# Gate and up projections by seven products of half blocks (Strassen), the residual kept in DRAM between uses, the down projection in three row groups

## The chip, the cores and the metric

One core of a Trainium2 chip runs the whole program. The metric is the device time of one execution, in microseconds (us). PE is the matrix engine (TensorE), ACT the scalar engine, DVE the vector engine, POOL the GpSimd engine; SP issues the DMAs.

## The reference, cut to what matters

Two layers over 576 tokens (64 of a running stream, 512 of a new one), everything in fp32. Each layer is FFN, mixer, FFN, with a norm before and after each; the four FFNs are what the change is about.

```python
D_MODEL, D_FF, DEPTH = 1024, 2816, 2

def _rmsnorm(x, g):
    y = x32 * lax.rsqrt(jnp.mean(x32 * x32, axis=-1, keepdims=True) + EPS)
    return (y * g.astype(jnp.float32)).astype(x.dtype)

def _swiglu(x, w_gate, w_up, w_down):
    return (jax.nn.silu(x @ w_gate) * (x @ w_up)) @ w_down

def _trunk(x, ...):
    for l in range(DEPTH):
        h = _rmsnorm(x, ng[0])
        x = x + 0.5 * _rmsnorm(_swiglu(h, ffn_w_gate[l, 0], ffn_w_up[l, 0], ffn_w_down[l, 0]), ng[1])
        h = _rmsnorm(x, ng[2])
        ...   # mixer: latent attention, HGRN2, chunk MLP, w_out
        x = x + _rmsnorm(mix, ng[3])
        h = _rmsnorm(x, ng[4])
        x = x + 0.5 * _rmsnorm(_swiglu(h, ffn_w_gate[l, 1], ffn_w_up[l, 1], ffn_w_down[l, 1]), ng[5])
```

## The kernel before

All activations are held transposed: a tile of 128 features by 576 tokens, so 1024 features are eight tiles (index k, 0 to 7). The residual `x` lives in eight fixed tiles of the pool `const`; everything else of this size comes from the pool `slots` (54 tiles of 128x576). The tokens are worked on in two column halves, `HALF`: 320 and 256 wide.

A product in fp32 is made of three matmuls (`three`, L138): weight and activation are each split into a high part of type fp32r and a low part. For a weight chunk of 128x1024 (`chunk`, L112) the load is a DMA on SP's queue into `wraw` (3 buffers), the high part `wh` an ACT copy (L120), the low part `wl` a DVE subtraction (L121); `whi` and `wlo` have 7 buffers each. `split` (L129) does the same to activations: `hh`/`hl` for the norm's output, `gh`/`gl` for the gated values. PSUM has 6 banks of tag `mm` and 2 of tag `sm`.

An FFN (`ffn`, L304) runs over 22 unit columns f of 128 hidden features. For each f, `unit` (L294) makes 48 matmuls for the gate and 48 for the up projection (8 k, 2 halves, 3 each), and `evac` takes them out of PSUM: times the norm's factor `rbc` (DVE L319), Silu (ACT L320), gate times up (DVE L321), split. The first two f, four chunks, are special: they run half by half (`units`, `together`), paced by the norm ahead of them, and their weights are loaded ahead. After 11 units the down projection takes the first 11 row blocks as one accumulation group and puts its result into `d` (SBUF); after 22 the second group is added. Chunks of down hold 256 columns and up to 4 row blocks. The last two column tiles of the second group run half by half, so that half 0's closing norm can be worked on while PE does half 1.

That norm is `post` (L221): the squared sums over features (ones-matmul, POOL power for the root), then per k on DVE `d` times gain times factor (L231), `x` + `d` (L234), and `pre` (L171) for the next stage: high part on ACT, low part on DVE (L136), squares on ACT, their sum `acc` on POOL (L182). Such small work is written as generators and interleaved into the matmul stream by counted PE time; the framework's scheduler then fixes each engine's order. Each engine runs its own order strictly in sequence.

Of the kernel before, what the change touches and what calls it, by code (L numbers as in the profile page):

```python
# [31 lines left out]
HALF = ((0, 320, (0, 1, 2)), (320, 256, (3, 4)))  # L32
# [11 lines left out]
class Net:  # L44
# [11 lines left out]
    def mul(self, out, lhsT, rhs, start, stop):  # L56
# [5 lines left out]
        self.nc.tensor.matmul(out, lhsT, rhs, start=start, stop=stop)  # L62
# [85 lines left out]
    def colsum(self, acc, tiles):  # L148
        ps = self.sm("ss")
        for j, i in enumerate(tiles):  # L150
            self.mul(ps[:, j:j + 1], acc[:, tcol(i):tcol(i) + P], self.ones[:, 0:1], start=True, stop=True)
        return ps

    def spread(self, r, tiles):
        ps = self.sm("bc")
        c = 0
        for j, i in enumerate(tiles):
            w = twid(i)
            self.flip(ps[:, c:c + w], r[:w, j:j + 1].to_broadcast([w, P]))
            c += w  # L160
        return ps

    def new_h(self):
        self.hh = [self.slot("hh", F32R) for _ in range(KT)]
        self.hl = [self.slot("hl", F32R) for _ in range(KT)]
        self.acc = self.slot("acc")
        self.rbc = self.slot("rbc")
        self.rn = self.small("rn", 5, 2)
        self.rn2 = self.small("rn2", 5, 2)

    def pre(self, half, k, gcol):  # L171
        nc = self.nc
        c0, n, _ = HALF[half]
        sl = slice(c0, c0 + n)
        xs = self.x[k][:, sl]
        self.split(self.hh[k][:, sl], self.hl[k][:, sl], xs, scale=gcol)
# [7 lines left out]
    def pre_stats(self, half, wait, sums=None):  # L184
        nc = self.nc
        c0, n, tiles = HALF[half]
        nt = len(tiles)
        t0 = tiles[0]
        rn, rn2, rbc, acc = self.rn, self.rn2, self.rbc, self.acc
        yield wait  # L190
        ps = self.colsum(acc, tiles) if sums is None else sums[:, t0:t0 + nt]
        m = self.small("m", 5)
# [5 lines left out]
        bc = self.spread(r, tiles)  # L198
        nc.scalar.activation(rbc[:, c0:c0 + n], bc[:, :n], AF.Copy)
        self.stats_done.add(half)  # L200

    def post_factor(self, half, acc, deferred):
        nc = self.nc
        tiles = HALF[half][2]
        nt = len(tiles)
        t0 = tiles[0]
        ps = self.colsum(acc, tiles)
        m = self.small("m", 5)
# [6 lines left out]
        p = self.small("p", 5)  # L215
# [5 lines left out]
    def post(self, half, d, acc, gpost, gpre, deferred):  # L221
        nc = self.nc
        c0, n, tiles = HALF[half]
# [17 lines left out]
    def after(self, half, d, acc, gpost, gpre, deferred):  # L241
# [1050 lines left out]
```

## Time and profile before

| | |
|---|---|
| device time, median of 3 runs | 2378.94 us (2377.78 to 2379.38) |
| span of the profiled execution, first to last instruction | 2377.5 us |
| PE busy | 2310.5 us, 97%, 16805 matmuls |
| DVE busy | 1146.5 us, 48% |
| ACT busy | 890.2 us, 37% |
| POOL busy | 217.9 us, 9% |
| mean granted PE clock | 0.991 of full speed |
| DMA | 182.76 MB, mean 77 GB/s |

The profile is of one execution; the page gives no other time of it than its span, which is 1.4 us under the median of the timed runs. "Busy" is the time in which an engine had at least one instruction running. The program's stages in the profiled execution: FFN 1 to about 440 us, mixer 1 to about 750 us, FFN 2 to about 1185 us, FFN 3 to about 1615 us, mixer 2 to about 1930 us, FFN 4 to the end.

### The profile page before, as it was taken

The numbers are of one execution on the slowest core, as the hardware profiler recorded it, in microseconds if no ns is written. First come the engines' busy times: TensorE is split into PE (matmuls) and PEld (weight loads), VectorE is DVE, ScalarE is ACT, GpSimd is POOL, SyncE is SP. The second block draws the span as 40 slices with busy tenths as digits, with TensorE's granted clock in tenths as the row PEclk, the third lists the DMA queues.
The fourth block names the chain that finished last, engine by engine and source line by source line (L and its number), as shares of the span: only waits on it lengthen the run. The fifth ranks groups of instructions, "written<-read, shape, count | busy, mean of one in ns | idle before, by whom it ended". The sixth has DMA issues, their size and how long they took to land.

```text
span 2377.5 us, 39904 instructions
## 1 busy us (share of the span) xinstructions
PE 2310.5 (97%) x16805; PEld 2257.1 (95%) x16805; DVE 1146.5 (48%) x2189; ACT 890.2 (37%) x1657; POOL 217.9 (9%) x230
## 2 busy tenths in 40 slices
PE   9999999998899999999999999999988999999998
PEld 8999999887799999999999999998877999999998
DVE  5332333788666532343473223337886574323333
ACT  6222222465555322232342222224646543222222
POOL 0000000333301000000020000003332020000000
PEclk9999999999999999999999999999999999999999
DMA  6223222122110422322232232222121214222211
GB/s 187 81 74 95 81 82 79 50 78 71 60 54 28 116 76 76 98 81 68 75 89 82 71 98 80 83 87 62 39 71 56 63 32 117 76 87 82 86 65 41
DMA packets 278344, 182.76 MB, mean 77 GB/s; under 512 B 13539, under 2 KB 270805, under 8 KB 278165
## 3 DMA queue, kind: packets, MB, share of 16 engines
q1 hardware_dynamic: 278164, 180.21, 25.3%
q8 instruction: 132, 2.16, 0.4%
q14 instruction: 48, 0.39, 0.1%
HBM read 175.96 MB, written 4.23 MB: 76 GB/s over the span
## 4 chain that ended last, share of the span: by engine, by line
PE 82%; DVE 10%; ACT 3%; POOL 3%; issue 2%; DMA 0%; SPq 0%; POOLq 0%; DVEq 0%; ACTq 0%
PE u L62 46%; PE d L62 24%; PE wo L62 4%; DVE zb L546 2%; PE sc L62 1%; DVE hl L136 1%; PE n L62 1%; DVE wl L121 1%; DVE x L234 1%; PE oT L62 1%; POOL gr L145 1%; PE q L62 1%; DVE d L231 1%; DVE at L561 1%; PE k L62 1%
## 5 line engine op out<-in xcount | busy, mean ns | idle before, releaser
L62 PE MATMUL u<-hl,wh 128*128 128x320 f32 (+1 forms) x3040 | 904.2, 298 | 2.6 <-DVE hl L136 2.6
L62 PE MATMUL u<-hh,wh 128*128 128x320 f32 (+1 forms) x3040 | 904.0, 299 | 1.9 <-DVE on L674 1.4
L62 PE MATMUL u<-hh,wl 128*128 128x320 f32 (+1 forms) x3040 | 902.4, 297 | 0.0
L120 ACT ACTIVATE wh<-wr 128x1024 fp32r<-128x1024 f32 (+1 forms) x334 | 344.5, 1032 | 756.3 <-issue 397.1
L121 DVE TENSOR_TENSOR wl<-wr,wh 128x1024 fp32r<-128x1024 f32 (+1 forms) x334 | 402.4, 1206 | 431.5 <-ACT wh L120 431.0
L62 PEld LDWEIGHTS u<-hl,wh 128*128 128x128 f32 x3040 | 580.0, 191 | 4.0 <-DVE hl L136 3.6
L62 PEld LDWEIGHTS u<-hh,wh 128*128 128x128 f32 x3040 | 578.6, 191 | 3.1 <-ACT mh L132 1.8
L62 PEld LDWEIGHTS u<-hh,wl 128*128 128x128 f32 x3040 | 579.7, 191 | 0.0
L62 PE MATMUL d<-gh,wh 128*128 128x320 f32 (+1 forms) x1408 | 418.7, 297 | 0.0
L62 PE MATMUL d<-gh,wl 128*128 128x320 f32 (+1 forms) x1408 | 417.0, 296 | 0.0
L62 PE MATMUL d<-gl,wh 128*128 128x320 f32 (+1 forms) x1408 | 416.7, 296 | 0.0
L62 PEld LDWEIGHTS d<-gl,wh 128*128 128x128 f32 x1408 | 267.3, 190 | 0.0
L62 PEld LDWEIGHTS d<-gh,wh 128*128 128x128 f32 x1408 | 267.2, 190 | 0.0
L62 PEld LDWEIGHTS d<-gh,wl 128*128 128x128 f32 x1408 | 267.2, 190 | 0.0
L321 DVE TENSOR_TENSOR t<-t,u 128x320 f32<-128x320 f32 (+1 forms) x176 | 79.6, 454 | 354.2 <-PE u L62 313.2
L145 POOL TENSOR_TENSOR p<-m,mhalf 128x3 f32<-128x3 f32 (+2 forms) x14 | 13.1, 936 | 1827.2 <-DVE m L212 1622.6
L319 DVE TENSOR_TENSOR t<-u,rbc 128x320 f32<-128x320 f32 (+1 forms) x176 | 79.8, 455 | 110.9 <-PE u L62 110.9
L320 ACT ACTIVATE t<-t 128x320 f32<-128x320 f32 (+1 forms) x176 | 76.5, 436 | 136.3 <-DVE t L319 136.3
L133 DVE TENSOR_TENSOR gl<-t,gh 128x320 fp32r<-128x320 f32 (+1 forms) x176 | 79.8, 455 | 39.7 <-ACT gh L132 39.7
L132 ACT ACTIVATE gh<-t 128x320 fp32r<-128x320 f32 (+1 forms) x176 | 76.6, 436 | 42.8 <-DVE t L321 42.8
L62 PE MATMUL n<-wh,hh 128*128 128x512 f32 (+1 forms) x240 | 92.2, 384 | 0.0
L62 PE MATMUL n<-wl,hh 128*128 128x512 f32 (+1 forms) x240 | 88.2, 368 | 0.0
(297 smaller groups left out, 2549.9 us busy)
## 6 DMA issues: line engine op xcount, KB each, us to landing
wr<-ffn_w_gate SPq DMA_DIRECT2D x88, 512.0 KB, 3.8
wr<-ffn_w_up SPq DMA_DIRECT2D x88, 512.0 KB, 3.8
wr<-ffn_w_down SPq DMA_DIRECT2D x64, 512.0 KB, 3.4
wr<-w_in SPq DMA_DIRECT2D x30, 512.0 KB, 3.8
wr<-ffn_w_down SPq DMA_DIRECT2D x32, 384.0 KB, 3.1
wr<-w_out SPq DMA_DIRECT2D x16, 512.0 KB, 3.4
xn<-x_prompt SPq DMA_DIRECT2D x4, 512.0 KB, 5.3
out_y_p<-xr SPq DMA_DIRECT2D x8, 256.0 KB, 2.1
```

The costliest lines, as they stand in the source:

```text
L62: self.nc.tensor.matmul(out, lhsT, rhs, start=start, stop=stop)
L120: nc.scalar.activation(hi[:, :a * b], raw[:, :a * b], AF.Copy)
L121: nc.vector.tensor_tensor(lo[:, :a * b], raw[:, :a * b], hi[:, :a * b].bitcast(F32), op=ALU.subtract)
L132: nc.scalar.activation(hi, src, AF.Copy)
L133: nc.vector.tensor_tensor(lo, src, hi.bitcast(F32), op=ALU.subtract)
L136: nc.vector.scalar_tensor_tensor(lo, src, scale, hi.bitcast(F32), op0=ALU.mult, op1=ALU.subtract)
L145: self.nc.gpsimd.tensor_tensor(out, m, self.mhalf[:, :n], op=ALU.pow)
L231: nc.vector.scalar_tensor_tensor(d[s][:, sl], d[s][:, sl], gpost[s], bc[:, :n], op0=ALU.mult, op1=ALU.mult)
L319: nc.vector.tensor_tensor(t[:, sl], pg[:, :n], self.rbc[:, sl], op=ALU.mult)
L320: nc.scalar.activation(t[:, sl], t[:, sl], AF.Silu)
L321: nc.vector.tensor_tensor(t[:, sl], t[:, sl], pu[:, :n], op=ALU.mult)
L546: nc.vector.tensor_tensor(zo, qv[rs, :, h:], ev[rs, :, h:], op=ALU.mult)
```

## The change

**Halves.** Both column halves are now 288 wide. The sums over columns use three runs of 128 columns per half (`RUNS`).

**Seven products.** The first two unit columns stay as they are. The other twenty go in ten pairs (f, f+1) through the new `seven`: the weight is seen as 2x2 blocks (features 0-3 or 4-7 of k, unit f or f+1), the activation as 2x2 blocks (k half, column half), and Strassen's scheme makes seven block products instead of eight. Each product is 24 matmuls of 288 columns (gate and up, 4 k, 3 parts), so a pair takes 168 matmuls where two units took 192. What is added for it: four DVE additions of weights per pair (L478, L480, L488, L497, 128x1024 each), splits of the seven weight tiles p1 to p7, and copies and additions on the way out of PSUM: ACT copies L487, L496, L503, DVE L511, L518, L520, L527, L529, L531, L536, L538, L539, two Silus of 576 columns. The weights come in four tiles per pair, each by two DMAs of 256 KB.

**Sums of activations.** The combinations t1 to t4 of activation blocks are made once per FFN by the new `combine`, after the second half of the first units: 16 ACT copies of 288 columns from `x`, 8 DVE additions of 576 columns, 8 splits of 576 columns.

**Down.** Three groups of 6, 8 and 8 row blocks; a chunk is 128 columns by the group's rows; the gated values are kept unsplit (`g`) and split at their group's start. The last group does its last three column tiles half by half.

**Residual.** `x` lives in `slots` (now 57; `const` loses its eight tiles): `stow` writes it to DRAM once the next stage's activations are made, `recall` loads it at the last group of down or of w_out. `wraw` has 6 buffers.

```diff
-HALF = ((0, 320, (0, 1, 2)), (320, 256, (3, 4)))
+W2 = T // 2
+HALF = ((0, W2), (W2, W2))
+RUNS = (((0, 64), (64, P), (W2 - P, P)), ((192, P), (320, P), (448, P)))
+GROUPS = ((0, 6), (6, 14), (14, 22))
...
+    def ffn(self, l, j, gpost, gpre, gain, nxt, packed):
...
+        ops = self.combine(gain)
+        self.until(lambda: 1 in self.stats_done)
+        for f in (0, 1):
+            evac(f, 1, o[2 * f][1], o[2 * f + 1][1])
+        for f in range(2, NF, 2):
+            self.seven(f, wg, wu, ops, g, rbc)
...
+        for a, (g0, g1) in enumerate(GROUPS):
+            first, last = a == 0, a == len(GROUPS) - 1
+            for f in range(g0, g1):
+                gh[f], gl[f] = self.slot("gh", F32R), self.slot("gl", F32R)
+                self.split(gh[f], gl[f], g.pop(f))
+            if last:
+                acc = self.slot("acc2")
+                self.recall()
...
+            tail = KT - 3 if last else KT
+            for m in range(tail):
+                run(m, self.cols(wd, m * P, P, g0, g1 - g0), (0, 1))
...
+    def combine(self, gain):
+        for q in range(2):
+            b = []
+            for kp in (q, q + 2):
+                for hf in range(2):
+                    c0, n = HALF[hf]
+                    t = self.slot("b")
+                    for e in range(2):
+                        k = 2 * kp + e
+                        nc.scalar.activation(t[:, e * n:(e + 1) * n], self.x[k][:, c0:c0 + n], AF.Copy, scale=gain[k])
+                    b.append(t)
+            b11, b12, b21, b22 = b
+            def part(name, src, scale=None):
+                o = self.slot("th", F32R), self.slot("tl", F32R)
+                self.split(*o, src, scale=scale)
+                ops[name].append(o)
+            nc.vector.tensor_tensor(b11, b11, b12, op=ALU.subtract)
+            part("t1", b11)
+            nc.vector.tensor_tensor(b11, b11, b22, op=ALU.add)
+            part("t2", b11, -1.0)
+            nc.vector.tensor_tensor(b22, b22, b12, op=ALU.subtract)
+            part("t3", b22)
+            nc.vector.tensor_tensor(b21, b11, b21, op=ALU.subtract)
+            part("t4", b21)
+        self.stow()
...
+    def seven(self, f, wg, wu, ops, g, rbc):
...
+        def product(w, b, ps, start):
+            for e in range(2):
+                for k in range(4):
+                    c = e * 512 + k * P
+                    h = ops[b][k // 2]
+                    s = slice((k % 2) * W2, (k % 2 + 1) * W2)
+                    self.three(ps[e][:, :W2], w[0][:, c:c + P], w[1][:, c:c + P], h[0][:, s], h[1][:, s],
+                               start and k == 0, k == 3, not start)
+                    self.tick()
...
+        a11, a21, a22 = load(0, f), load(0, f + 1), load(4, f + 1)
+        p1 = part(a11)
+        s = self.wraw.tile([P, 1024], F32, name=self.name("ws"), tag="wr")
+        nc.vector.tensor_tensor(s, a21, a22, op=ALU.add)
+        p5 = part(s)
+        nc.vector.tensor_tensor(a21, a21, a11, op=ALU.add)
+        a12 = load(4, f)
+        X = [self.mm("X"), self.mm("X")]
+        product(p1, "b11", X, True)
+        s1 = [self.slot("s1"), self.slot("s1")]
+        for e in range(2):
+            nc.scalar.activation(s1[e][:, A], X[e][:, :W2], AF.Copy)
+        nc.vector.tensor_tensor(s, s, a11, op=ALU.add)
+        p6 = part(s)
+        Q = [self.mm("Q"), self.mm("Q")]
+        product(p5, "t1", Q, True)
+        s5 = self.slot("s5")
+        for e, h in enumerate((A, B)):
+            nc.scalar.activation(s5[:, h], Q[e][:, :W2], AF.Copy)
+        nc.vector.tensor_tensor(s, s, a12, op=ALU.add)
+        p3 = part(s)
+        product(p6, "t2", X, False)
+        for e in range(2):
+            nc.scalar.activation(s1[e][:, B], X[e][:, :W2], AF.Copy)
+        p7 = part(a21)
+        product(p3, "b22", Q, False)
+        g[f] = self.slot("g")
+        t = [g[f], s1[1]]
+        for e in range(2):
+            nc.vector.tensor_tensor(t[e][:, B], s1[e][:, B], Q[e][:, :W2], op=ALU.add)
+        p2 = part(a12)
+        product(p7, "t3", X, False)
+        for e, h in enumerate((A, B)):
+            nc.vector.tensor_tensor(s5[:, h], s5[:, h], X[e][:, :W2], op=ALU.add)
+        nc.vector.scalar_tensor_tensor(g[f + 1][:, B], s5[:, A], -1.0, rbc[:, B], op0=ALU.mult, op1=ALU.mult)
+        p4 = part(a22)
+        R = [self.mm("R"), self.mm("R")]
+        product(p2, "b21", R, True)
+        for e in range(2):
+            nc.vector.tensor_tensor(t[e][:, A], s1[e][:, A], R[e][:, :W2], op=ALU.add)
+        nc.vector.tensor_tensor(t[0], t[0], rbc, op=ALU.mult)
+        nc.scalar.activation(t[0], t[0], AF.Silu)
+        nc.vector.tensor_tensor(g[f], t[0], t[1], op=ALU.mult)
+        product(p4, "t4", X, False)
+        nc.vector.scalar_tensor_tensor(u[:, A], X[0][:, :W2], -1.0, rbc[:, A], op0=ALU.mult, op1=ALU.mult)
+        nc.scalar.activation(u, u, AF.Silu)
+        nc.vector.scalar_tensor_tensor(u[:, B], s5[:, B], -1.0, u[:, B], op0=ALU.mult, op1=ALU.mult)
+        nc.vector.scalar_tensor_tensor(u[:, A], X[1][:, :W2], -1.0, u[:, A], op0=ALU.mult, op1=ALU.mult)
...
+    def stow(self):
+        for k in range(KT):
+            self.nc.sync.dma_start(self.xd[k], self.x[k])
+    def recall(self):
+        self.x = [self.slot("x") for _ in range(KT)]
+        for k in range(KT):
+            self.nc.sync.dma_start(self.x[k], self.xd[k])
...
-                tc.tile_pool(name="wraw", bufs=3) as net.wraw, \
+                tc.tile_pool(name="wraw", bufs=6) as net.wraw, \
-                tc.tile_pool(name="slots", bufs=54) as net.slots, \
+                tc.tile_pool(name="slots", bufs=57) as net.slots, \
```

**DVE at the start of the third FFN.** Before, from the last low part of the norm's output (the first row) on, DVE prepares one weight chunk (`wl`) after another, with the evacuation of the first units between them.

```order
L136 SCALAR_TENSOR_TENSOR hl_12064<-x_83,colg,hh_12056 128x256
L319 TENSOR_TENSOR t_12394<-u_12188,rbc_12066 128x320
L193 TENSOR_SCALAR m_12499<-ss_12496 128x2
L121 TENSOR_TENSOR wl_12660<-wr_12657,wh_12659 128x1024
L196 TENSOR_TENSOR rn_1715_12068<-rn_12067 128x2
L321 TENSOR_TENSOR t_12394<-t_12394,u_12189 128x320
L121 TENSOR_TENSOR wl_12716<-wr_12713,wh_12715 128x1024
L133 TENSOR_TENSOR gl_12393<-t_12394,gh_12392 128x320
```

Now the same place goes on, after that last low part and the evacuation of the first units' half 0, with `combine`. These rows are its end: t1's second tile (`tl_12840`), t2's and t3's (`tl_12845`, `tl_12850`), and between them the low parts of p3 (`wl_12966`), p7 (`wl_12996`) and p2 (`wl_13027`).

```order
L497 TENSOR_TENSOR ws_12890<-ws_12890,wr_12897 128x1024
L436 TENSOR_TENSOR b_12826<-b_12826,b_12829 128x576
L139 TENSOR_TENSOR tl_12840<-b_12826,th_12839 128x576
L341 TENSOR_TENSOR g_12682<-g_12682,u_12689 128x288
L438 TENSOR_TENSOR b_12826<-b_12826,b_12835 128x576
L139 TENSOR_TENSOR wl_12966<-ws_12890,wh_12965 128x1024
L142 SCALAR_TENSOR_TENSOR tl_12845<-b_12826,th_12844 128x576
L440 TENSOR_TENSOR b_12835<-b_12835,b_12829 128x576
L442 TENSOR_TENSOR b_12832<-b_12826,b_12832 128x576
L139 TENSOR_TENSOR wl_12996<-wr_12880,wh_12995 128x1024
L139 TENSOR_TENSOR tl_12850<-b_12835,th_12849 128x576
L139 TENSOR_TENSOR wl_13027<-wr_12897,wh_13026 128x1024
```

What stood there before, only weight chunks for units to come, is now behind eight additions and eight low parts of activations; `tl_12840` is the twenty-second row after the last low part of the norm's output (`hl_12662`), `wl_13027` the thirty-first.

**PE at the same place.** These are the first pair's second product (Q), then the first five matmuls of its sixth product (R, by p2), then the third (X, by p6 with t2); brackets name the engine a row waits for.

```order
L68 MATMUL Q_12936<-th_12839,wl_12893 128x288
L68 MATMUL Q_12936<-th_12839,wh_12892 128x288
L68 MATMUL Q_12936<-tl_12840,wh_12892 128x288
L68 MATMUL Q_12936<-th_12839,wl_12893 128x288
L68 MATMUL R_13062<-hh_12458,wh_13026 128x288 [waits Activation_49]
L68 MATMUL R_13062<-hl_12459,wh_13026 128x288
L68 MATMUL R_13063<-hh_12458,wh_13026 128x288 [waits DVE_49]
L68 MATMUL R_13063<-hl_12459,wh_13026 128x288
L68 MATMUL R_13062<-hh_12458,wl_13027 128x288 [waits DVE_49]
L68 MATMUL X_12900<-th_12812,wh_12931 128x288 [waits Activation_49]
L68 MATMUL X_12900<-tl_12813,wh_12931 128x288
L68 MATMUL X_12900<-th_12812,wl_12932 128x288
```

R's fifth matmul reads `wl_13027`, and all of X, which the order puts behind it, comes after that.

**DVE in a steady pair.** Before, two units' worth of DVE rows: weight low parts of 1024 columns and evacuations of 320 and 256.

```order
L319 TENSOR_TENSOR t_12645<-u_12521,rbc_12066 128x320
L121 TENSOR_TENSOR wl_12968<-wr_12965,wh_12967 128x1024
L321 TENSOR_TENSOR t_12645<-t_12645,u_12593 128x320
L121 TENSOR_TENSOR wl_13038<-wr_13035,wh_13037 128x1024
L133 TENSOR_TENSOR gl_12644<-t_12645,gh_12643 128x320
L319 TENSOR_TENSOR t_12651<-u_12522,rbc_12066 128x256
L321 TENSOR_TENSOR t_12651<-t_12651,u_12594 128x256
L133 TENSOR_TENSOR gl_12644<-t_12651,gh_12643 128x256
L319 TENSOR_TENSOR t_12771<-u_12663,rbc_12066 128x320
L121 TENSOR_TENSOR wl_13094<-wr_13091,wh_13093 128x1024
L321 TENSOR_TENSOR t_12771<-t_12771,u_12719 128x320
L121 TENSOR_TENSOR wl_13164<-wr_13161,wh_13163 128x1024
```

Now, a part of one pair: weight additions (L478, L480, L488), low parts, and evacuations of the pair before.

```order
L478 TENSOR_TENSOR ws_13378<-wr_13368,wr_13371 128x1024
L139 TENSOR_TENSOR wl_13375<-wr_13365,wh_13374 128x1024
L480 TENSOR_TENSOR wr_13368<-wr_13368,wr_13365 128x1024
L139 TENSOR_TENSOR wl_13381<-ws_13378,wh_13380 128x1024
L488 TENSOR_TENSOR ws_13378<-ws_13378,wr_13365 128x1024
L139 TENSOR_TENSOR wl_13420<-ws_13378,wh_13419 128x1024
L511 TENSOR_TENSOR g_13267<-s_2052_13170,Q_13179 128x288
L497 TENSOR_TENSOR ws_13378<-ws_13378,wr_13385 128x1024
L511 TENSOR_TENSOR s_2053_13171<-s_2053_13171,Q_13180 128x288
L518 TENSOR_TENSOR s_2058_13205<-s_2058_13205,X_13144 128x288
L139 TENSOR_TENSOR wl_13454<-ws_13378,wh_13453 128x1024
L520 SCALAR_TENSOR_TENSOR g_13300<-s_2058_13205,rbc_12323 128x288
```

A pair now has eleven rows of 1024 columns where two units had four.

## Rows read from the trace of the kernel before

**Rows 1.** The page, part 1: busy time, share, instructions.

```profile
PE 2310.5 (97%) x16805; PEld 2257.1 (95%) x16805; DVE 1146.5 (48%) x2189; ACT 890.2 (37%) x1657; POOL 217.9 (9%) x230
```

**Rows 2.** The page, part 4: the chain that ended last, by engine.

```profile
PE 82%; DVE 10%; ACT 3%; POOL 3%; issue 2%; DMA 0%; SPq 0%; POOLq 0%; DVEq 0%; ACTq 0%
```

**Rows 3.** The chain in order of time: start, duration, what.

```profile
34.69 125.28 PE u L62 x948
159.96 70.40 PE d L62 x528
230.36 140.80 PE u L62 x1056
371.16 64.16 PE d L62 x476
```

**Rows 4.** Stretches: length, busy PE, PEld, DVE, ACT, POOL, then clock, DMA share, GB/s.

```profile
34.60:434.00 399.40, 399.40 (x3000) 399.40 (x3000) 144.74 (x222) 112.61 (x184) 0.00 (x0) 1.00 0.29 88
...
1192.00:1222.00 30.00, 26.79 (x191) 26.02 (x191) 26.78 (x49) 13.82 (x29) 12.06 (x13) 0.94 0.30 86
1207.60:1210.60 3.00, 1.12 (x9) 1.02 (x9) 2.25 (x6) 1.94 (x5) 2.49 (x4) 0.98 0.00 0
1210.60:1213.80 3.20, 3.20 (x17) 3.20 (x16) 3.20 (x5) 0.02 (x1) 1.13 (x2) 0.50 0.06 16
```

**Rows 5.** Timeline of PE in down: start, duration, instruction.

```profile
210.20 0.31 PE L62 MATMUL d<-gh,wh 128*128 128x320 f32 x1
...
210.64 0.28 PE L62 MATMUL d<-gh,wh 128*128 128x256 f32 x1
...
211.00 0.31 PE L62 MATMUL d<-gh,wh 128*128 128x320 f32 x1
```

**Rows 6.** Groups of instructions by shape, 240 to 365 us: busy, mean ns, idle before.

```profile
L121 DVE TENSOR_TENSOR wl<-wr,wh 128x1024 fp32r<-128x1024 f32 x18 | 22.1, 1225 | 15.4 <-ACT wh L120 15.4
L120 ACT ACTIVATE wh<-wr 128x1024 fp32r<-128x1024 f32 x18 | 19.1, 1060 | 63.3 <-issue 44.9 <-PE u L62 18.4
L132 ACT ACTIVATE gh<-t 128x320 fp32r<-128x320 f32 x10 | 4.5, 453 | 0.0
```

**Rows 7.** Timeline of DVE at the start of the third FFN.

```profile
1196.21 0.86 DVE L231 SCALAR_TENSOR_TENSOR d<-d,colg,bc 128x256 f32<-128x256 f32 x2
1197.00 0.41 DVE L234 TENSOR_TENSOR x<-x,d 128x256 f32<-128x256 f32 x1
1197.33 0.47 DVE L231 SCALAR_TENSOR_TENSOR d<-d,colg,bc 128x256 f32<-128x256 f32 x1
...
1210.50 1.75 DVE L121 TENSOR_TENSOR wl<-wr,wh 128x1024 fp32r<-128x1024 f32 x1
1212.17 0.47 DVE L136 SCALAR_TENSOR_TENSOR hl<-x,colg,hh 128x256 fp32r<-128x256 f32 x1
...
1215.71 1.22 DVE L121 TENSOR_TENSOR wl<-wr,wh 128x1024 fp32r<-128x1024 f32 x1
1216.84 0.49 DVE L133 TENSOR_TENSOR gl<-t,gh 128x320 fp32r<-128x320 f32 x1
1217.24 0.48 DVE L319 TENSOR_TENSOR t<-u,rbc 128x320 f32<-128x320 f32 x1
```

**Rows 8.** Timeline of POOL there.

```profile
1209.44 1.73 POOL L182 TENSOR_TENSOR acc<-acc,sq 128x256 f32<-128x256 f32 x2
```

**Rows 9.** The chain at the same place.

```profile
1209.52 0.63 PE bc L67 x3
1210.15 2.17 PE u L62 x12
1212.32 0.65 PE ss L62 x4
1212.96 9.48 PE u L62 x72
```

**Rows 10.** The stretch table for tile u alone (columns as in rows 4, without POOL).

```profile
1203.70:1212.95 9.25, 6.43 (x43) 6.05 (x43) 0.38 (x1) 0.00 (x0) 0.87 0.00 1
```

**Rows 11.** DMA issues: count, KB each, median us from issue to landing.

```profile
wr<-ffn_w_gate SPq DMA_DIRECT2D x88, 512.0 KB, 3.8
...
wr<-ffn_w_down SPq DMA_DIRECT2D x64, 512.0 KB, 3.4
```

**Rows 12.** The chain's last piece.

```profile
2373.19 1.32 DVE xr L1113 x2
```

More of the change, by code (lines that the diff above doesn't have):

```diff
@@ L61, in mul @@
             self.t += max(4 * n / 2400, 0.107)
-        self.nc.tensor.matmul(out, lhsT, rhs, start=start, stop=stop)
+        self.nc.tensor.matmul(out, lhsT, rhs, start=start, stop=stop, skip_group_check=onto)
     def flip(self, out, src):
@@ L155, in spread @@
+    def spread(self, r, half, runs=None):
+        runs = runs or RUNS[half]
         ps = self.sm("bc")
[L156 to L165, printed above, removed]
+        b = runs[0][0]
+        for j, (c, w) in enumerate(runs):
+            self.flip(ps[:, c - b:c - b + w], r[:w, j:j + 1].to_broadcast([w, P]))
+        c0, n = HALF[half]
+        return ps[:, c0 - b:c0 - b + n]
@@ L197, in pre_stats @@
         yield 3.11
-        bc = self.spread(r, tiles)
-        nc.scalar.activation(rbc[:, c0:c0 + n], bc[:, :n], AF.Copy)
+        bc = self.spread(r, half, None if sums is None else tuple((tcol(i), twid(i)) for i in range(2 * half, 2 * half + nt)))
+        nc.scalar.activation(rbc[:, c0:c0 + n], bc, AF.Copy)
         self.stats_done.add(half)
+        if sums is not None and half == 0:
+            yield 1.0
+            ps = self.sm("ru")
+            self.mul(ps[:, 0:1], rbc[0:1, W2 - P:W2], self.ones[0:1, 0:1], start=True, stop=True)
+            nc.vector.tensor_copy(rn[:, 2:3], ps[:, 0:1])
+            nc.vector.tensor_tensor(rn2[:, 2:3], rn[:, 2:3], rn[:, 2:3], op=ALU.mult)
     def post_factor(self, half, acc, deferred):
         nc = self.nc
[L204 to L208, printed above, removed]
+        nt = 3
+        t0 = 3 * half
+        ps = self.colsum(acc, RUNS[half])
+        m = self.small("m", 6)
         if deferred:
@@ L222, in post @@
         nc = self.nc
-        c0, n, tiles = HALF[half]
+        c0, n = HALF[half]
         sl = slice(c0, c0 + n)
@@ new lines, in ffn @@
+            tail = KT - 3 if last else KT
+            for m in range(tail):
+                run(m, self.cols(wd, m * P, P, g0, g1 - g0), (0, 1))
+            if last:
+                chs = [self.cols(wd, m * P, P, g0, g1 - g0) for m in range(tail, KT)]
+                self.ahead = [self.cols(*q) for q in nxt]
+                for hf in (0, 1):
+                    for m in range(tail, KT):
+                        run(m, chs[m - tail], [hf])
+                    self.after(hf, d, acc, gpost, gpre, (r, r2), packed)
```

294 lines of the change are left out of this document (158 added, 136 removed).

## The prediction

> **What bounds the kernel now.** I read the page's busy times first: PE is busy 97% of the span, DVE 48%, ACT 37% [rows 1]. Then the chain that ended last: 82% of it is PE, 10% DVE [rows 2]. In order of time the chain shows where PE alone counts: in an FFN it runs in pieces of 64 to 141 us without a break, gate and up, down, gate and up, down [rows 3]. The stretch table says the same of the whole FFN: 34.6 to 434 us has 399.40 us of PE in 399.40, DVE 144.74, ACT 112.61, POOL 0.00, at full granted clock [rows 4]. So an FFN's time is its number of matmuls times the time of one. Between stages it is otherwise: 1192 to 1222 us has PE at 26.79 of 30 and DVE at 26.78 of 30, clock 0.94 [rows 4]; there DVE has no slack.
>
> A matmul's time: in down, the starts of one set (three of 320 columns, three of 256) are 210.20, 210.64, 211.00 [rows 5]: 146.7 ns and 120 ns each, which is (n + 32) / 2.4 GHz. The new width lies between: 288 columns take 133.3 ns. Two equal halves cost the same as two unequal ones, so the halves by themselves change nothing on PE; the chain agrees, with 70.40 us for 528 matmuls of down, 133.3 ns on average [rows 3].
>
> **What is removed.** Ten pairs per FFN, 192 matmuls before, 168 after: 24 x 133.3 ns = 3.2 us per pair, 25.6 us to 22.4 us. Four FFNs: 40 x 3.2 = **-128.0 us**, if PE stays the bound in a pair.
>
> **Does PE stay the bound?** Per pair, by start-to-start times of DVE, which are a little under the durations (a `wl` of 1024 columns 1215.71 to 1216.84, 1.13 us; a 320 tile 0.40 us, a 256 tile 0.33, so 288 about 0.37 [rows 7]): seven low parts and four weight additions, 11 x 1.15 = 12.7; ten evacuations of 288, 3.7 (a few with a scalar operand, 0.39 at 256 columns [rows 7], add 0.3); two of 576, twice 0.74, 1.5. That is 18.2 us; with a wait of DVE for ACT before the sixth tile's low part (the addition L488 is followed at once by the `wl` that needs an ACT copy of its result, 1060 ns [rows 6]) 19.3, under 22.4. By mean durations, 1225 ns for a `wl` [rows 6], the eleven are 13.5 and the sum is 20.1. The additions have no row of their own; the nearest is the `wl` subtraction, the same operation on as many columns, and I take its time. ACT: seven copies at 1060 ns, six evacuations at about 0.44 (453 ns at 320 columns [rows 6]) and two Silus at about 0.7: 11.5 us. DMA: 2 MB per 22.4 us is 94 GB/s where this stretch now moves 88 [rows 4]; loads of such rows land in 3.8 us [rows 11], and each pair's weights are prepared a pair ahead. So the term stands, with 2.3 to 4.2 us of DVE to spare per pair.
>
> What could upset it is shown by one row: a `wl` took 1.75 us, 1.67 to the next start, while POOL added two accumulators of 256 columns [rows 7, 8]. The Trainium skill, "SBUF — State Buffer", section "Who interferes with whom", says that a DVE instruction with two SBUF inputs contends with a GpSimd instruction that reads SBUF, under an exclusive lock; all eleven wide DVE rows of a pair are of that kind, so it speaks against moving work from PE to them; by that rule with POOL busy the sum would be that of the DVE rival below, with POOL idle it stays. In the pairs POOL has nothing to do: 0.00 us in 399 [rows 4]. The row's price comes back as a rival.
>
> **What is added at each FFN's start.** `combine` puts 16 copies of 288 and 8 splits on ACT (about 12 us) and 8 additions and 8 low parts of 576 on DVE (about 12 us) into the stretch where DVE is already full. I replay the queues in program order for FFNs 2 to 4, with t = 0 at half 1's first `d` row, 1196.21 before [rows 7]. Before, the last `hl` ends at 16.4 and PE runs without a break from 1212.96 [rows 9]. After, the same rows at 288 columns end at about 17.5. PE had 43 of half 1's 96 matmuls started by 1212.95 [rows 10]; some 55 are left at t = 16.75, then X by p1 (24) and Q's first 12: 91 x 133.3 ns = 12.1, broadcasts 0.5, and 0.8 that the 72 matmuls took beyond 120 ns each [rows 9] make 30.1, where Q needs t1's second tile. DVE needs for that, after the last `hl`, the 22 rows up to `tl_12840`: three of 1024 (3.4), ten of 576 (7.3), seven of 288 (2.6), small ones (0.3), 13.6 together; waits for ACT, whose eight copies of the second b tiles stand ahead of the high part that `tl_12840` needs, add about 1.5. So 32.6: **2.5 us of stall**. Then PE has 14 matmuls of Q and R (1.9), and R's fifth needs `wl_13027`, nine rows further: three of 1024, five of 576, one of 288, 7.5 us, at 40.0 instead of 34.5: **5.5 us of stall**. X behind it would start no sooner than about 39.6 by ACT either, where the copies that empty X stand behind four weight copies and three splits. From there PE has 91 matmuls (12 us) before its next row that DVE or ACT could hold up, and DVE only its steady work. Per FFN 8.0; the first FFN, whose norm has no `post` ahead of it, about 6.5 by the same replay. Sum **+30.5**. Bounds: if ACT never made DVE wait, 1.0 + 5.5 = 6.5 per FFN; if the six wide rows there cost 1.67 each, 11.1. Sums 26 and 44.
>
> A stall also costs clock: after 1.9 us without a matmul (PE busy 1.12 of 3.00 from 1207.6) the granted clock is 0.50 (1.2 GHz) from 1210.6 to 1213.8 [rows 4], where 3.2 us do the work of 1.6. I count one such stretch per FFN, **+6.4**; none or two would be 0 or 12.8.
>
> **Smaller terms.** Down: a new group boundary per FFN (the third group replaces none); at group 1's first chunks the weight low parts wait for buffers that PE is still reading, with gated splits behind them: about 1 us each, **+4** (0 to 8). Its matmuls are as many as before, and its rows of 512 bytes load like the gate's (3.8 against 3.4 us [rows 11]), 6.4 us of PE per chunk cover them. The end: half 1 of the last norm has six row pieces, not four, at 0.66 us [rows 12]: **+1.5**; more transposes at the start, half hidden, +0.5. Transitions: half 0's norm is covered by 72 matmuls of 133.3 ns (9.6 us) instead of 66 of 120 ns (7.9) in FFNs, 72 of 120 (8.6) in mixers; three at 1.7 and two at 1.0 would be 7.1 at most; I take **-4**. Stow and recall: 6 x 2 x 2.36 MB; a stow waits only for the last `x` row, which comes before `combine`'s copies; a recall is issued a whole group before its first use (8 x 48 matmuls, 51 us, in down; half of that in w_out); nothing on the path. Cover gone, 2.36 MB at the rate of one load, 512 KB in 3.8 us [rows 11], is 17 us.
>
> **Sum.** 2377.5 - 128.0 + 30.5 + 6.4 + 4 + 2 - 4 = 2288.4 us of span; the median of timed runs lies 1.4 above the profiled span: **2290 us**, 3.7% faster. Its own range, from the bounds of combine (-4.5, +13.5), clock (6.4 either way), boundaries and transitions (4 each), taken together by their squares: 2280 to 2306.
>
> **Rivals.**
> *FFN starts hidden.* If the stalls were taken up by work ordered otherwise, only the small terms remain: 2377.5 - 128 + 2 + 1.4 = 2253 us. For it: DVE is idle most of a pair before. Against it: each engine runs in order, and `wl_13027` is behind 31 rows of DVE.
> *DVE bounds the pairs.* This one ends slower. If the wide rows cost 1.75 us, as the one beside POOL did [rows 7], a pair is 19.3 + 5.5 + 1.1 = 25.9 us, 3.5 us over 22.4: 40 x 3.5 = 140 on 2290, **2430 us**. It decides from the point where a pair takes 22.4 + 89/40 = 24.6 us, 1.64 us per wide row; with 1.67 it would be 2394. Against it: POOL is idle there, and 18 of 18 `wl` average 1225 ns [rows 6].
> *The residual arrives late.* If SP's queue, in order, holds recalls behind weight loads that wait for buffers, or the freed slots come late, each of the six uses costs up to 17 us; at a third to half of that, 2290 + 45, some 2335 us. Against it: the covers above.
> *Waits between the products.* PSUM tiles are reused within a pair: X is copied out (ACT, two rows of 0.44) before t2 is added to it. Q's 24 matmuls (3.2 us) cover that; if an ACT weight copy (1.06) and another stand ahead each time, 0.5 us per product, 3 of them per pair: 40 x 1.5 = 60, 2350 us. Against it: before, PE also shares two banks and an ACT queue and does not wait once in 399 us [rows 4].
>
> **How the numbers follow.** Chances: as forecast 0.68; starts hidden 0.09; residual late 0.08; waits between products 0.11; DVE bound 0.04. I predict the likeliest, 2290. The range must leave out no more than 2 in 10: down to 2262 it takes in most of a partly hidden start, up to 2330 the upper bounds and a part of the late residual. A measurement here tells changes over 0.2% (about 5 us) from none. Only the DVE rival, and it only beyond its break-even, ends slower: 0.03; the same 0.01; faster 0.96.
>
> **What would show it.** Right: 960 fewer matmuls of gate and up; pairs of 22.4 us with PE unbroken; two PE gaps after each FFN's first pair begins, of about 2.5 us (before `tl`) and 5.5 us (before `wl` of p2), a stretch of half clock behind them; DVE about 80% busy in pairs, L478 near 1.2 us. Wrong: DVE rows of 1024 columns over 1.5 us in pairs; PE waiting for DVE in every pair; PE waiting for a DMA after `recall`; starts without gaps.

## The result and the profile after

The changed kernel takes 2313.46 us (median of 4 runs, 2312.85 to 2313.92) where the kernel before, on the same chip, takes 2379.16: ratio 0.9722 (0.9708 to 0.9736). The gain is 65.7 us; 89 were forecast. The profiled execution spans 2311.6 us at a mean clock of 0.979 (before 2377.5 and 0.991).

The page, part 1 and the engines' shares of part 4's chain, as in [rows 1, 2]:

```profile
PE 2217.3 (96%) x15892; PEld 2155.0 (93%) x15892; DVE 1594.7 (69%) x2671; ACT 1114.0 (48%) x1945; POOL 225.4 (10%) x230
...
PE 76%; DVE 14%; ACT 4%; issue 3%; POOL 3%; DMA 0%; SPq 0%; POOLq 0%; DVEq 0%; ACTq 0%
```

PE is busy 93 us less, the span is 66 us shorter: PE now stands idle some 27 us more than before. The stretches of two pairs (columns as in [rows 4]) and the chain over the length of one pair:

```profile
98.67:121.07 22.40, 22.40 (x170) 22.40 (x170) 18.45 (x24) 10.74 (x15) 0.00 (x0) 1.00 0.33 94
121.07:143.47 22.40, 22.40 (x170) 22.40 (x170) 17.80 (x24) 10.81 (x15) 0.00 (x0) 1.00 0.33 95
```

```profile
73.87 6.40 PE X L68 x48
80.27 3.20 PE Q L68 x24
83.47 3.20 PE X L68 x24
86.67 3.20 PE Q L68 x24
89.87 3.20 PE X L68 x24
93.07 3.20 PE R L68 x24
```

In the pairs everything is as forecast: 24 matmuls in 3.20 us, a pair in 22.40 without a break, DVE at 18.1 us, ACT at 10.8, 94 GB/s. The groups by shape, 98.67 to 210.67 us (five pairs), show that the new additions cost what the `wl` of [rows 6] cost:

```profile
L139 DVE TENSOR_TENSOR wl<-wr,wh 128x1024 fp32r<-128x1024 f32 x20 | 24.4, 1221 | 0.6 <-ACT wh L138 0.4
L139 DVE TENSOR_TENSOR wl<-ws,wh 128x1024 fp32r<-128x1024 f32 x15 | 18.4, 1226 | 16.9 <-ACT wh L138 16.9
...
L478 DVE TENSOR_TENSOR ws<-wr,wr 128x1024 f32<-128x1024 f32 x5 | 6.1, 1226 | 1.8 <-issue 1.8
```

The second row also shows DVE's main wait in a pair: 16.9 us in five pairs, 3.4 us each, spread over three rows, for the ACT copy of a sum of weights. The waits of PE, as line waited for, then us in total, times, longest:

```profile
PE R L68 <- DVE wl L139: 12.8, 4, 3.5
...
PE ss L68 <- POOL acc L198: 7.6, 5, 2.0
PE bc L73 <- POOL rn L151: 7.5, 6, 2.1
PE Q L68 <- ACT th L138: 7.1, 4, 2.6
PE ss L68 <- DVE acc L315: 4.2, 5, 1.6
...
PE R L68 <- ACT wh L138: 3.3, 4, 1.4
PE d L68 <- ACT gh L138: 2.7, 4, 0.7
...
PE Q L68 <- DVE tl L139: 1.4, 4, 0.4
```

`R` and `Q` wait where it was said, once per FFN. Their four rows make 24.6 us. `Q`'s wait was forecast for DVE's `tl`; most of it (7.1 of 8.5 us) ends with ACT's `th`. The second FFN's start on the timeline, three rows of PE:

```profile
781.71 0.53 PE L68 MATMUL Q<-th,wh 128*128 128x288 f32 x2 [2.60 <-ACT th L138]
...
785.57 0.61 PE L68 MATMUL R<-hh,wh 128*128 128x288 f32 x1 [0.53 <-ACT wh L138]
...
789.80 0.61 PE L68 MATMUL R<-hh,wl 128*128 128x288 f32 x1 [2.90 <-DVE wl L139]
```

And the stretch around them, then one with the third FFN's first pair, and the stretch of mixer 1 between its last `u` and w_out (same columns):

```profile
780.00:800.00 20.00, 14.43 (x80) 13.50 (x81) 19.46 (x24) 12.69 (x21) 0.00 (x0) 0.74 0.33 97
783.20:793.40 10.20, 6.78 (x28) 6.08 (x27) 10.20 (x12) 6.63 (x12) 0.00 (x0) 0.50 0.37 108
1203.00:1206.40 3.40, 3.40 (x14) 3.40 (x15) 3.40 (x4) 0.00 (x0) 0.00 (x0) 0.51 0.59 168
...
602.10:660.90 58.80, 52.98 (x338) 48.36 (x339) 36.96 (x102) 39.52 (x98) 8.26 (x7) 0.91 0.19 56
```

DVE has no slack at the start (19.46 of 20), and PE runs at 1.2 GHz (0.50) behind the gaps. The last row is what the forecast did not have. The same stretch of the kernel before:

```profile
621.40:676.40 55.00, 48.98 (x339) 44.93 (x338) 37.25 (x102) 39.04 (x98) 8.07 (x7) 1.00 0.20 61
```

The mixer's code computes the same. PE has as many matmuls, to one, and stands idle as long (5.8 and 6.0 us), but is busy 4.0 us longer, at clock 0.91 instead of 1.00. By stages, from the times of the matmuls that begin and end them (us, one profiled execution each; the lower rows are those of the experiments below):

```
               start  FFN1  mixer1  FFN2   FFN3  mixer2  FFN4   end    span
before          14.5  428.3  310.8  431.7  433.2  312.9  436.8   9.3  2377.5
after           14.3  407.2  316.8  413.5  412.9  317.2  418.6  11.0  2311.6
no combine      15.0  399.6  316.6  401.5  402.9  317.4  408.0  11.0  2271.9
plain units     14.2  429.9  314.6  433.1  436.8  319.1  439.9  11.0  2398.7
halves alone    17.0  430.2  315.5  432.1  433.5  319.4  437.3  11.0  2396.2
plain, fixed x  16.6  432.1  315.4  433.0  435.3  316.2  437.7  11.0  2397.2
four plain      13.8  402.2  316.4  406.8  407.4  319.0  410.5  11.0  2287.2
```

The four FFNs gain 77.8 us, not the 90 or so that the sum gives them; the mixers lose 10.3, where it has no loss. Mixer 1 and mixer 2 as a whole, before and then after (columns as in [rows 4]):

```profile
443.00:753.60 310.60, 288.51 (x1947) 265.36 (x1947) 224.68 (x521) 174.72 (x364) 83.58 (x82) 0.99 0.20 60
1618.60:1931.40 312.80, 289.69 (x1947) 266.75 (x1947) 227.13 (x525) 174.62 (x364) 80.85 (x82) 0.98 0.20 59
```

```profile
421.70:738.30 316.60, 295.80 (x1955) 271.95 (x1954) 224.49 (x521) 173.61 (x361) 83.10 (x81) 0.97 0.24 72
1564.90:1882.00 317.10, 297.02 (x1955) 273.02 (x1955) 227.16 (x525) 173.70 (x361) 81.64 (x81) 0.96 0.23 71
```

PE stands idle 4.3 us less than before in the two together and is busy 14.6 us longer, at a lower clock and with only 8 small matmuls more in each: the mixers lose clock, not waiting time.

### The profile page after: what moved, and what is told of

Read it like the earlier page. It is cut to its first block, busy times and chain, and to the rows that moved or that the text cites. A ratio compares the mean times of both kernels' runs of the same rounds, so it can differ in the third digit from the quotient of the medians.

```text
span 2311.6 us, 39493 instructions
## 1 busy us (share of the span) xinstructions
PE 2217.3 (96%) x15892; PEld 2155.0 (93%) x15892; DVE 1594.7 (69%) x2671; ACT 1114.0 (48%) x1945; POOL 225.4 (10%) x230
## 4 chain that ended last, share of the span: by engine, by line
PE 76%; DVE 14%; ACT 4%; issue 3%; POOL 3%; DMA 0%; SPq 0%; POOLq 0%; DVEq 0%; ACTq 0%
PE d L68 23%; PE X L68 22%; PE Q L68 11%; PE R L68 6%; PE wo L68 4%; PE u L68 3%; DVE zb L706 2%; PE n L68 2%; DVE hl L142 2%; DVE x L256 1%; PE sc L68 1%; DVE d L253 1%; DVE wl L127 1%; DVE wl L139 1%; PE q L68 1%
## 5 line engine op out<-in xcount | busy, mean ns | idle before, releaser
L68 PE MATMUL d<-gh,wh 128*128 128x288 f32 x1408 | 413.5, 297 | 2.7 <-ACT gh L138 2.7
L68 PE MATMUL d<-gl,wh 128*128 128x288 f32 x1408 | 413.9, 295 | 0.0
L68 PE MATMUL d<-gh,wl 128*128 128x288 f32 x1408 | 412.7, 294 | 0.0
L127 DVE TENSOR_TENSOR wl<-wr,wh 128x1024 fp32r<-128x1024 f32 (+2 forms) x174 | 203.4, 1173 | 175.9 <-ACT wh L126 175.1
L68 PE MATMUL X<-th,wh 128*128 128x288 f32 x960 | 286.8, 299 | 0.0
L68 PE MATMUL X<-tl,wh 128*128 128x288 f32 x960 | 285.5, 297 | 0.0
L68 PE MATMUL X<-th,wl 128*128 128x288 f32 x960 | 284.5, 296 | 0.0
L139 DVE TENSOR_TENSOR wl<-wr,wh 128x1024 fp32r<-128x1024 f32 x160 | 194.7, 1222 | 8.2 <-ACT wh L138 6.8
L68 PEld LDWEIGHTS X<-th,wl 128*128 128x128 f32 x960 | 183.1, 191 | 0.0
L68 PEld LDWEIGHTS X<-tl,wh 128*128 128x128 f32 x960 | 182.8, 190 | 0.0
```

Source lines behind the costliest of these rows:

```text
L127: nc.vector.tensor_tensor(lo[:, :a * b], raw[:, :a * b], hi[:, :a * b].bitcast(F32), op=ALU.subtract)
L139: nc.vector.tensor_tensor(lo, src, hi.bitcast(F32), op=ALU.subtract)
```

## The experiments

Two questions: what of the 128 us goes to the FFN starts, where `combine` works, and what to the rest of the change (halves, groups, residual), which the forecast held to be nearly free.

**`combine` left out.** The pairs take parts of `h` in place of t1 to t4; the kernel is otherwise the changed one.

```diff
...
+            for name, key in (("t1", (q, 0)), ("t2", (q, 1)), ("t3", (q + 2, 1)), ("t4", (q + 2, 0))):
+                ops[name].append(self.h[key])
```

> Leaves out the sums of activations: t1 to t4 are taken as the norm's output parts themselves, so the ACT copies, the additions and the splits of combine are gone; the seven products and all else stay. Theory A (most of what the change gave back lies at the start of each FFN, where PE waits for combine's rows on ACT and DVE and then runs at half clock): the waits for th, tl and the low part of p2 (24.6 us in all) go, and the half-clock stretches behind them (about 10 us of loss), so about 2278 us, 2268 to 2288. Theory B (the loss is spread over the pairs, the mixers and the residual's transfers): no more than 10 us faster than the changed kernel, 2303 or more.

2273.32 us (2270.78 to 2275.8), ratio 0.9553 (0.9538 to 0.9568). The waits for `th`, `tl` and `wl` are gone from the table, and the FFNs, taken together, gain 40.2 us against the changed kernel; the mixers stay as long. So `combine` costs 40 us.

**The seven products undone,** all else kept:

```diff
-        ops = self.combine(gain)
+        self.stow()
...
-        for f in range(2, NF, 2):
-            self.seven(f, wg, wu, ops, g, rbc)
+        for f in range(2, NF):
+            pg = self.unit(self.cols(wg, f * P))
+            pu = self.unit(self.cols(wu, f * P))
+            for hf in (0, 1):
+                evac(f, hf, pg[hf], pu[hf])
```

> Undoes the seven products alone: all 22 unit columns as plain units of 192 matmuls per two, no combine; equal halves, the residual in DRAM and the three row groups of down stay. Theory A: nothing is lost at the FFN starts, so the rest of the change costs only its small terms against the kernel before: mixers 10, down 2, end 2, which gives 2393 us (2388 to 2398). If the losses in the mixers come with the seven products (buffers, order), it is the time of before, 2379 us (2376 to 2384). If the residual's transfers held things up, over 2400 us.

2395.54 us (2394.45 to 2400.8), 1.0071 (1.0055 to 1.0087): the rest of the change costs 16 us. Its profiled execution, near the top of its runs, has 9.7 us of it in the FFNs and 10.0 in the mixers. This kernel and the one without `combine` differ by the seven products alone: 122.2 us by the medians, 127.7 in the FFNs of the table.

**Which part of the rest.** The same with the residual in fixed tiles again, no `stow` and `recall`, 54 slots and 3 `wraw` buffers:

```diff
-        self.x = [self.slot("x") for _ in range(KT)]
+        self.x = [const.tile([P, T], F32, name=f"x{k}", tag=f"x{k}") for k in range(KT)]
...
```

> The run with plain units once more (2396 us), and the residual back in eight fixed tiles: no stow, no recall, slots 54 and wraw 3 as before. What is left of the change are the equal halves and the three row groups of down. If the residual's transfers or its share of the slots cost the 10 us of the mixers: 2383 to 2387 us. If the equal halves do (another order of the small work in the mixers, with waits at other places and half clock behind them): 2393 to 2397.

2398.37 us (2398.09 to 2398.94), 1.0077 (1.006 to 1.0094): no gain, so the residual in DRAM costs nothing that shows. Then the kernel before with the equal halves and what hangs on them (three runs of columns per half, the norm's output for the FFNs in tiles of two k by one half):

```diff
-HALF = ((0, 320, (0, 1, 2)), (320, 256, (3, 4)))
+HALF = ((0, W2), (W2, W2))
...
```

> The kernel before with the equal halves alone: 288 and 288 columns, three runs of columns per half for the sums; the FFN as before in plain units with two groups of down between them, the residual in fixed tiles, slots 54, wraw 3. The prediction priced the equal halves at nothing on PE and 2 us at the two ends. If they carry what the run with plain units and fixed residual lost (2398 against 2379.5): 2391 to 2397 us, with both mixers 3 to 5 us longer each. If the three groups of down, with the order of work around them, carry it: 2380 to 2385.

2396.85 us (2392.89 to 2397.93), 1.0068 (1.005 to 1.0086): the equal halves alone make the kernel 17 us slower. In the table of stages 11.2 of its 18.7 us are in the mixers, 3 in the FFNs, 4 at the two ends. The same place of mixer 1 as above, where PE is busy 2.2 us longer than before and idle 1.5 us longer:

```profile
626.70:685.40 58.70, 51.14 (x339) 46.88 (x340) 36.95 (x102) 39.52 (x98) 8.25 (x7) 0.94 0.18 56
...
635.80:642.60 6.80, 4.86 (x15) 3.77 (x15) 3.73 (x18) 3.27 (x10) 1.33 (x1) 0.50 0.13 28
```

One thing that differs there is an order. PE's timeline of the kernel before has six `v` matmuls of 512 columns between the last `q` and the transposes `tp` of `ck`, here three of them:

```profile
628.36 0.47 PE L62 MATMUL v<-wh,cth 128*128 128x512 f32 x1
628.67 0.39 PE L62 MATMUL v<-wl,cth 128*128 128x512 f32 x1
628.90 0.40 PE L62 MATMUL v<-wh,ctl 128*128 128x512 f32 x1
629.15 1.25 PE L62 MATMUL ss<-ones,accq 128*128 128x1 f32 x10
```

With equal halves (this kernel; the changed one reads alike) the scheduler puts them later, PE has small work and gaps there, and the granted clock is 0.50 from 635.80 on (second row above):

```profile
633.46 0.38 PE L73 MATMUL tp<-ident_c,on 128*128 128x128 f32 x2
634.40 1.47 PE L68 MATMUL ss<-ones,accq 128*128 128x1 f32 x12 [0.56 <-DVE ml L139]
636.56 0.45 PE L73 MATMUL tp<-ident_c,ck 128*128 128x128 f32 x1 [0.69 <-DMA ck<-cache_mla_ckv]
```

That this order brings the half clock is read from the rows and not shown: there are also twelve `ss` for ten, and a kernel with the old order and equal halves was not run. That the clock is what the mixers lose has more for it: between two kernels with equal halves, mixer 2 takes 314.7 us at a mean clock of 0.98 (four plain units and the order of need, below) and 319.3 us at 0.96 (this one), and all of the difference is PE's busy time (293.4 and 298.1 us) on the same matmuls.

**The price of the start: order.** `combine` in the order of need (t1's two tiles, then t2's, and so on):

```diff
...
+        block("b11", 0, 0)
+        block("b12", 0, 1)
+        sums("b11", "b11", "b12", ALU.subtract, "t1")
+        block("b22", 2, 1)
+        sums("b11", "b11", "b22", ALU.add, "t2", -1.0)
...
```

> Same work as the changed kernel, but combine makes t1 for both tiles first, then t2, t3, t4, instead of all four for the first tile and then for the second. Theory A with the order as cause: the waits of Q for th and tl (8.5 us) go, but five matmuls of R stay ahead of X on PE and still wait for the low part of p2, the 31st DVE row behind the norm's last: that wait takes over most of it. 2300 to 2311 us. If only the amount of work counts: 2313, within 3. If the order alone is the cause: 2285.

2303.09 us (2301.97 to 2306.53), 0.9682 (0.9664 to 0.9699): 10 us better. `Q` waits no more; `R`'s wait for `wl` grew from 12.8 to 15.5 us. The scheduler had put the whole of `R` ahead of the next `X`, so next `R` was pinned to its place in the program for the first pair:

```diff
...
+        if pin:
+            self.tc.keep_in_program_order(ins)
...
-        product(p2, "b21", R, True)
+        product(p2, "b21", R, True, f == first)
```

> As the one before (sums in the order of their use), and the first pair's R held in program order on PE, behind the product that the code writes ahead of it. Theory A with the order of R as the second cause: both waits mostly go, 4 x 6 to 9 us: 2277 to 2292 us. If the amount of DVE and ACT work decides and not the order: 2305 to 2313 us, with the waits moved to X, Q and their weights.

2312.37 us (2309.93 to 2313.49), 0.9715 (0.97 to 0.9731): the order of `R` is not the second cause; the time is that of the other forecast, in which the amount of work on DVE and ACT decides. The first row of PE's waits:

```profile
PE X L68 <- ACT s L493: 29.7, 4, 8.8
```

The stall moved to the copy of `X` out of PSUM, which stands on ACT behind copies for weights, `b` and `th`. The prediction had named this as the next limit. And with half 1's broadcast of the norm's factor issued at once:

```diff
-        yield 3.11
+        yield 3.11 if sums is not None or half == 0 else 0.0
...
```

> Ten pairs, sums in the order of their use, and the transposes that spread half 1's norm factor (bc) issued as soon as the factor is there; PE's order then has 43 unit matmuls ahead of them instead of 58. ACT's copy of bc stands in ACT's row ahead of combine's rest, and in the trace of the changed kernel ACT and DVE stand idle 3.6 and 1.6 us until PE reaches bc. If that ring (PE late, so ACT and DVE late, so PE late) counts: 1.5 to 2.5 us per FFN for FFNs 2 to 4, 2295 to 2300 us. If not: 2303, within 3.

2302.48 us (2301.46 to 2305.16), 0.9677 (0.9661 to 0.9693): no change against the order of need alone.

**The price of the start: time to do it in.** Unit columns 2 and 3 are left plain, which gives DVE and ACT 25.6 us of matmuls to work under, and nine pairs follow:

```diff
-        for f in range(2, NF, 2):
+        for f in (2, 3):
+            pg = self.unit(self.cols(wg, f * P))
+            pu = self.unit(self.cols(wu, f * P))
+            for hf in (0, 1):
+                evac(f, hf, pg[hf], pu[hf])
+        for f in range(4, NF, 2):
```

> As the changed kernel, but the unit columns 2 and 3 are also plain units, put between combine and the first pair: nine pairs per FFN. PE gets 25.6 us of matmuls that need nothing of combine, and gives back 3.2 us per FFN. Theory A (the start's waits, and the half clock behind them, are the cost of combine coming just before its first use): 4 x (9 to 11 less, 3.2 more), 2278 to 2292 us, no waits of PE for th, tl or p2. If the rows of combine have to be paid for wherever they stand: 2313 + 13 = 2326 us.

2283.76 us (2283.14 to 2288.93), 0.9601 (0.9586 to 0.9615): 30 us better than the changed kernel, though it gives up four pairs' 12.8. The FFNs of its profiled execution, the slowest of four, are 25.3 us shorter, so 38 with those 12.8 (by the medians 29.7, so 42): about all that `combine` costs. The waits of the first pairs are gone. With the order of need on top:

```diff
+        for f in range(4, NF, 2):
...
+        sums("b11", "b11", "b12", ALU.subtract, "t1")
...
```

> The same with combine's sums in the order of their use. With 25.6 us of cover the order should no longer matter: within 4 us of the run before. If it still matters, ACT or DVE is behind for longer than the cover: 5 to 10 us faster than the run before.

2286.4 us (2285.42 to 2290.37), 0.961 (0.9596 to 0.9625): the order no longer matters.

**The clock at the start.** 20 and 28 idle matmuls of 288 columns stand in the first pair's gaps, in the program one set behind `X`, one behind `Q`; nothing reads them:

```diff
+        def fill(n):
+            ps = self.sm("fl")
+            for j in range(n):
+                ins = self.nc.tensor.matmul(ps[:, :W2], p1[0][:, :P], ops["b11"][0][0][:, :W2], start=True, stop=True)
...
+        if f == 2:
+            fill(20)
...
+        if f == 2:
+            fill(28)
```

> The changed kernel with idle matmuls that nobody reads in the first pair's two waits: 20 of 288 columns behind X by p1, 28 behind Q, 2.7 and 3.7 us at full clock. The waits are as long as DVE and ACT make them; PE is busy in them. If the half clock behind the waits costs what I read from the trace (the 24 matmuls of X after them take 4.5 us and not 3.2): 1 to 2 us per FFN, 2305 to 2310 us, with no half-clock stretch at the first pair. If the clock there is hidden behind DVE anyway, or the fillers are too long: 2313 to 2320.

2304.53 us (2302.32 to 2307.0), 0.9683 (0.9669 to 0.9698): 9 us better, though PE has more to do. The second FFN's start:

```profile
780.00:800.00 20.00, 18.18 (x133) 17.72 (x134) 19.60 (x25) 10.94 (x18) 0.00 (x0) 1.00 0.36 105
```

The clock is 1.00 where the changed kernel has 0.74 over the same 20 us. So some 9 of the 40 us go with the clock; the FFNs of the profiled execution, the slowest of four, are 6.6 us shorter.

**DVE's margin in the pairs.** The first sum of weights is made five times over, four wide rows more per pair:

```diff
-        nc.vector.tensor_tensor(s, a21, a22, op=ALU.add)
+        for _ in range(5):
+            nc.vector.tensor_tensor(s, a21, a22, op=ALU.add)
```

> The changed kernel with four more DVE additions of 128x1024 per pair (the first sum of weights is made five times). DVE was busy 18.25 us of a pair's 22.40. Theory: PE bounds the pair with 4.1 us of DVE to spare, of which up to 3.4 are waits for ACT; 4 x 1.13 = 4.5 us more use it up, and 40 pairs get 0.4 to 3.5 us longer: 2330 to 2450 us; a pair in the trace then has DVE over 95% busy. If DVE's spare time were larger than it looks: 2313. It prices the rival in which DVE bounds the pairs.

2409.8 us (2404.39 to 2413.11), 1.0123 (1.0107 to 1.014): 96 us more, 2.4 per pair, which turns the gain into a loss. A stretch within its pairs, the largest wait of PE in the whole execution, and DVE's in that stretch:

```profile
150.00:200.00 50.00, 45.72 (x322) 44.32 (x322) 43.77 (x53) 21.02 (x30) 0.00 (x0) 0.97 0.30 85
```

```profile
PE Q L68 <- ACT wh L138: 36.7, 26, 1.4
```

```profile
DVE wl L139 <- ACT wh L138: 5.5, 7, 1.2
```

DVE is busy 88%, not the 95% that was expected. Four rows at 1.22 us are 4.9 us, of which 2.4 show: a pair had about 2.5 us to spare, less than the 4.3 by which DVE's busy time lies under 22.40. Of DVE's 6.2 idle us in this stretch 5.5 are waits for ACT's `wh`; that DVE and ACT hold each other up in the chain sum, high part, low part is read from these waits.

**One addition on POOL** (L480), which is idle in the pairs:

```diff
-        nc.vector.tensor_tensor(a21, a21, a11, op=ALU.add)
+        nc.gpsimd.tensor_tensor(a21, a21, a11, op=ALU.add)
```

> The changed kernel with one of the four weight additions of a pair (a21 + a11) on POOL in place of DVE. It asks whether DVE's wide rows cost 1.7 us beside POOL, as one row did in the trace of before, and what the time is then. By the row (a POOL addition of 256 columns took 0.87, so 1024 some 2.5 to 3.5 us): one or two wide DVE rows of a pair lie beside POOL's and take 1.7 to 3 us; DVE loses one row and is held for about as long: 18 to 21 us of 22.4, PE stays the bound, 2309 to 2318 us. If POOL's hold is longer than its own row or hits every wide row: over 2330.

2312.27 us (2310.81 to 2313.35), 0.9715 (0.9701 to 0.973): no change. The timeline of POOL and DVE in one pair:

```profile
102.46 2.72 POOL L480 TENSOR_TENSOR wr<-wr,wr 128x1024 f32<-128x1024 f32 x1 [15.33 <-DVE ws L478]
...
103.20 3.07 DVE L139 TENSOR_TENSOR wl<-wr,wh 128x1024 fp32r<-128x1024 f32 x1
```

The `wl` beside it takes 3.07 us instead of 1.22: it ends 1.09 us after POOL's row does (105.18), as if it had begun then. The Trainium skill, "SBUF — State Buffer", section "Who interferes with whom", has an exclusive lock between a DVE instruction with two SBUF inputs and a GpSimd instruction that reads SBUF; this pair of rows agrees. What DVE hands over it pays back in waiting.

## Why the prediction was right in direction and 23 us short

**Products, -128.0: right.** Pairs take 22.40 us, and taking the products out costs 122 to 128. The profile counts 913 matmuls fewer: 960 fewer for gate and up, and 47 small ones more that equal halves add (16852 in the run with the halves alone, 16805 before). DVE at 18.1 us per pair was forecast as 18.2. But the forecast counted one wait of DVE for ACT in a pair, 1.1 us, where there are three with 3.4; what a pair has to spare is about 2.5 us, at the lower end of the forecast 2.3 to 4.2. The DVE rival did not come, but its mechanism is real: at 2.4 us more per pair the kernel is slower than before (four more additions); its break-even was put at 2.2.

**`combine`, +30.5 and +6.4: right in mechanism, near in size partly by luck.** 36.9 forecast, 40.2 by leaving it out. The waits were both named in place: 2.1 us per FFN for `Q` (2.5 forecast), 4.0 for `R` (5.5). So 24.6 instead of 30.5; the clock was put at 6.4 and is near 9 by the idle matmuls. Some 6.6 us remain, which have no term and were not taken apart; they make up for the waits' 5.9 too many.

**Halves, 0: wrong, and the largest miss.** "The halves by themselves change nothing on PE" counted columns at one clock. It is true of the columns and false of the kernel: equal halves alone cost 17 us, some 11 of them in the mixers. There PE falls to 1.2 GHz in stretches where it did not before, behind an order of small work that has changed; that the order is the reason was not tested. The mixers' 10.3 us have no term in the sum.

**Transitions, -4: not to be seen.** The longer cover of half 0's norm was to take up waits for POOL's root. The waits of `bc` for `rn` and of `ss` for either `acc` come to 19.3 us in the table above; the kernel before has 15.6:

```profile
PE bc L67 <- POOL rn L145: 10.2, 6, 1.9
PE ss L62 <- DVE acc L292: 5.4, 5, 1.3
```

`bc` does wait less, by 2.7 us, and `ss` now waits 7.6 us for POOL's `acc`, which was not in the table before: what was late next was not asked. Whether the transitions gain or lose stays open: the same three rows come to 15.1 us in the run with one addition on POOL, which takes the changed kernel's time, and to 11.8 us with the halves alone.

**Down, +4, the ends, +2, the residual, 0: right.** Down breaks once per FFN at a new group, between these two pieces of the chain, by 1.06 us (4.2 us in all), of which `gh` explains up to 0.7:

```profile
278.67 38.01 PE d L68 x285
...
317.74 94.50 PE d L68 x708
```

The ends cost 1.4 us. No wait of PE in its table of waits is for a recalled `x`, and the residual held in SBUF gives nothing back. Waits between the products, the likeliest rival, do not show: PE is unbroken in the pairs.

**The sum again.** By the table of stages the FFNs are at -128 + 40.2 + 9.7 (plain units) = -78.1, measured -77.8; with the mixers at +10.3 and the ends at +1.4 that is -66.4 against a difference of spans of 65.9. By the medians, each run against the kernel before on its own chip, -128 + 40.9 + 15.6 = -71.5 against -65.7: the 6 us between are those by which the products come out at 122 instead of 128, and by which the runs with plain units differ among themselves. Of the 9.7 us in the FFNs, 3 are the halves', 4 to 5 the three groups' (plain units with fixed `x` against halves alone) and the rest the residual's; these small differences come from single executions.

The sum's own range was 2280 to 2306 us, and the measured time lies above it. It lies in the wider range, 2262 to 2330, whose upper part was there for a late residual that did not come; that the mixers' loss, which has no term in the sum, fell into it is luck.

## What to carry to other kernels

Work that saves matmuls is paid for where its operands are made: look for the stretch in which the other engines have no slack, and give them matmuls to work under; here two plain units per FFN bought about all of the 40 us back, at the price of 12.8 us of products, while the order of that work bought 10 and pinning `R` on PE lost 9 of these again. An edit that "changes nothing" in columns can still change the order and the granted clock elsewhere, so compare every stage, not only the edited one, and price each stretch at the clock it is granted. An engine that takes turns with another can be at its limit before it is full: DVE was at 88% where four more rows made every pair longer.

## What was not expected of the hardware

In a stretch of mixer 1, 338 matmuls of the changed kernel took 52.98 us of PE where 339 took 48.98 before, with as much idle time, at clock 0.91 instead of 1.00. Idle matmuls in gaps shortened the kernel by 9 us. A DVE row beside a POOL row took 3.07 us instead of 1.22, so an idle POOL was no reserve here.
